# One room for all weight tiles, side work at fixed places, and unsplit last tiles in a two-layer trunk with experts

## The chip, the core and the metric

The kernel runs on one core of a Trainium2 chip. The metric is the device time of one execution in microseconds. A core has a matrix engine (TensorE, PE in the profile, with its weight loads as PEld), a vector engine (VectorE, DVE), a scalar engine (ScalarE, ACT), GpSimd (POOL) and SyncE (SP), which here only starts transfers. Each engine goes through its own list of instructions in order and waits for others by semaphores. Sixteen DMA engines carry the transfers.

## The reference

256 tokens of width 1024 go through two layers. Each has a mixer (four kinds of attention side by side, `w_in` and `w_out`) and a feed-forward part. In layer 0 that is dense, in layer 1 each token goes to 2 of 8 experts:

```
def swiglu(t, w_gate, w_up, w_down):
    return (jax.nn.silu(t @ w_gate) * (t @ w_up)) @ w_down

def moe_swiglu(h, router, w_gate, w_up, w_down):
    t = h.reshape(B * S, D)
    logits = (t @ router).astype(jnp.float32)
    top_val, top_idx = lax.top_k(logits, TOP_K)
    gates = jax.nn.softmax(top_val, axis=-1)
    combine = jnp.sum(jax.nn.one_hot(top_idx, N_EXPERTS) * gates[..., None], axis=1)
    out = jnp.zeros_like(t)
    for e in range(N_EXPERTS):
        out = out + combine[:, e:e + 1] * swiglu(t, w_gate[e], w_up[e], w_down[e])
```

Everything is float32; D = 1024, the hidden width F = 3584. A last RMSNorm follows. The experts' weights alone are 8 x 3 x 1024 x 3584 x 4 bytes, 352 MB of the 430 MB that the program reads.

## The kernel before

**Tiles and halves.** All large weights are a list of tiles, `units`, numbered in the order of use. The experts' part begins at tile 72. The hidden width of an expert is worked on in two halves of 1792, so there are 16 halves, i = 0 to 15. `expert_units` (L107) lists for each half eight gate tiles and eight up tiles (128 rows x 1792, 896 KB each) and then the seven down tiles (256 x 1024, 1 MB) of the half before. So half 0 is tiles 72 to 87, half 1 is 88 to 103, the down tiles of half 0 are 104 to 110, and so on; half 15's down tiles stand alone at the end and are cut finer (five whole ones and three pieces of 512 columns with 4, 2 and 2 row blocks).

**What is done to a tile.** A tile comes as float32 into a stage. For fp16 products it is split: ACT writes hi = fp16(512 w) (`high_part`, L169), DVE writes lo = fp16(512 w - hi) (`low_part`, L172). Tokens are split likewise, so each 128x128 block of weights takes three fp16 products with 96 token columns: hi with both parts of the tokens (L1157, L1158), lo with the first (L1161). In the down stage these are L1190 and L1192. The last gate tile and the last up tile of a half (`k == KD - 1`) are not split: TensorE multiplies them as float32 (L1151), which a record shows as two products for a block.

**Places.** Nine ring buffers (`stgp`, 8,320 bytes a partition) and four fixed places (e0, e2, e3, xn: buffers of earlier stages, 8,192 bytes) hold raw tiles, six hi and six lo buffers (`cvtp`) hold split ones. `load_next` (L156) starts one transfer on SP each time a raw place becomes free: after a tile's lo, or, for a tile that isn't split, after its products. A tile that leaves a fixed place hands it to the next tile in the list.

**What sets the order.** The schedule is manual: each engine's order is the order in which the code issues. `done` (L228) ends a tile's use and lets `go` split on until `ahead` tiles (six in the experts' part, `N_CVT`) are split past the one in use. The last nine tiles (`brisk`) are split in two pieces each.

**Around the tiles.** `gate_up` (L1164) does a half's gate and up tiles, then DVE and ACT finish the hidden values in three column spans: product (L1178), its fp16 part (L1179), the rest (L1180); this is "the three-part step". `down` (L1196) multiplies the half before. Other experts' side work is in a queue `side`: for the next expert, `slots` and five gathers of its tokens (copies at L1087); for the expert before, two transposes of its sum (`turn_back`, L1213 to L1216) and four additions into x (`scatter`, L1222 on TensorE, L1224 on DVE). One entry is taken after each up tile from the sixth on and after each down tile. `closing` (L1291) does the down tiles of half 15, the last transposes (tags e0, e1 : `yte`), additions and sums of squares. The final gain is loaded into a ring buffer after the last tile.

Of the kernel before, what the change touches and what calls it, by code (L numbers as in the profile page):

```python
# [20 lines left out]
P = 128  # L21
# [20 lines left out]
NB = FH // P  # L42

# [26 lines left out]
def hybrid_trunk_kernel(ctx: ExitStack, tc: tile.TileContext, a: dict, out: bass.AP, dbg=None):  # L70
# [4 lines left out]
    stgp = ctx.enter_context(tc.tile_pool(name="stgp", bufs=N_STG))  # L75
    cvtp = ctx.enter_context(tc.tile_pool(name="cvtp", bufs=N_CVT))
# [30 lines left out]
    def expert_units(sets, tail=False):  # L107
# [3 lines left out]
        for i in range(len(seq) + 1):  # L111
# [4 lines left out]
            if i > 0:  # L116
                (_, _, wd), h = seq[i - 1]
                ends = tail and i == len(seq)
                got += [(rows(wd, h * FH + r * P, 2, 0, D), 2, D, False) for r in range(0, NB - 4 if ends else NB, 2)]
                if ends:  # L120
                    r0 = h * FH + (NB - 4) * P
                    got += [(rows(wd, r0 + r * P, kt, c0, 512), kt, 512, False) for r, kt, c0 in ((0, 4, 0), (0, 2, 512), (2, 2, 512))]
        return got

    MLA_KT = (2, 2, 4)
    units = []
    for layer in range(DEPTH):
# [10 lines left out]
        if layer % 2 == 0:  # L138
            units += dense_units(a["dense_w_gate"][j], a["dense_w_up"][j], a["dense_w_down"][j])
        else:  # L140
            sets = [(a["moe_w_gate"][j, e], a["moe_w_up"][j, e], a["moe_w_down"][j, e]) for e in range(NE)]
            units += expert_units(sets, layer == DEPTH - 1)

    class Stream:


        def __init__(self, units, stage_tile, part_tiles, ahead):
            self.units, self.stage_tile, self.part_tiles = units, stage_tile, part_tiles
            self.loaded = self.split = self.low = self.used = 0
            self.stage, self.place, self.high, self.ready = {}, {}, {}, {}  # L150
# [3 lines left out]
            self.brisk = 0  # L154

        def load_next(self, place=None):  # L156
            u = self.loaded
            if u < len(self.units):
                src, kt, n, _ = self.units[u]
                stg = self.stage_tile(u, place)  # L160
                self.place[u] = place
                nc.sync.dma_start(stg[:, : kt * n].rearrange("p (k n) -> p k n", k=kt), src)
                self.stage[u] = stg
                self.loaded += 1
            elif place is None and self.last:
                self.last.pop()()
# [7 lines left out]
        def split_next(self):  # L174
# [7 lines left out]
            m = self.units[u][1] * self.units[u][2]  # L182
            self.high[u] = self.part_tiles[0](u)
            self.split += 1
            if u >= len(self.units) - self.brisk:
                self.low_until(u)
                lo = self.part_tiles[1](u)
# [8 lines left out]
        def top_up(self):  # L196

            if self.split < min(len(self.units), self.used + N_CVT) and not self.units[self.split][3]:
                u = self.split
                self.high[u] = self.part_tiles[0](u)  # L200
                self.high_part(u, slice(0, self.units[u][1] * self.units[u][2]))
                self.split += 1

        def low_until(self, end):
            while self.low < end:
                if self.units[self.low][3]:
                    self.ready[self.low] = (self.stage[self.low],)
                    self.low += 1
                    continue
                lo = self.part_tiles[1](self.low)  # L210
                self.low_part(self.low, lo, slice(0, self.units[self.low][1] * self.units[self.low][2]))
                self.low_done(lo)

        def low_done(self, lo):
            u = self.low
            _, kt, n, _ = self.units[u]
            self.stage.pop(u)
            self.ready[u] = tuple(z[:, : kt * n].rearrange("p (k n) -> p k n", k=kt) for z in (self.high.pop(u), lo))
            self.low += 1
            self.load_next(self.place.pop(u))  # L220

        def get(self, later=0):
            while self.split <= self.used + later:
                self.split_next()
# [3 lines left out]
        def done(self):  # L228
# [3 lines left out]
            if self.units[u][3]:  # L232
                self.stage.pop(u)
                self.load_next(self.place.pop(u))
# [6 lines left out]
        def go(self):  # L241
            while not self.held and self.split < min(len(self.units), self.used + self.ahead):
                self.split_next()
# [10 lines left out]
    parts = (  # L254
        lambda u: cvtp.tile([P, 2080], F16, tag="hi", name=f"hi{u}"),
        lambda u: cvtp.tile([P, 2080], F16, tag="lo", name=f"lo{u}"),
    )

    def stage_tile(u, place):
        if place:  # L260
            return (ext if place[0] == "e" else com).tile([P, 2048], F32, tag=place, name=f"stg{u}")
# [1141 lines left out]
```

## Time and profile before

| | |
|---|---|
| Time, median of 3 | 1368.21 us (1367.33 to 1368.56) |
| Profiled execution, its own time | 1368.37 us |
| Its span | 1366.6 us |
| PE, PEld busy | 1277.3 us (93%), 1134.5 us (83%) |
| DVE, ACT busy | 1079.5 us (79%), 898.2 us (66%) |
| POOL busy | 32.4 us (2%) |
| Read from memory | 430.41 MB, 316 GB/s over the span |

The span lies 1.77 us below the execution's own time. The busy shares are means over stages of different kinds: the first layer and the second layer's mixer up to about 500 us, the experts from there to 1347 us, and a short end of additions and the last norm. The experts' part is to be read by itself, in windows, and its two ends apart from its middle.

### The profile page before, as it was taken

Reading aid. Unit: us, or ns where it says so; the run is one execution under the profiler, and the core shown is the slowest. Engines: PE = TensorE matmul, PEld = TensorE weight load, DVE = VectorE, ACT = ScalarE, POOL = GpSimd, SP = SyncE. Lnnn points to the kernel's source line nnn. Section 1 sums busy time; section 2 is a strip of 40 time slices with the busy share of each in tenths; the row PEclk is TensorE's granted clock in tenths of the full one; section 3 lists DMA queues with packets and bytes.
Section 4 is the critical chain, followed back from the end, with each engine's and each line's share of the span. In section 5 each row is a group of like instructions: output and inputs, shape, how many; then the busy total and the mean of one; then the engine's idle time right before and its main releaser. Section 6 shows DMA issues by size and latency. Waiting matters only on the chain.

```text
span 1366.6 us, 43224 instructions
## 1 busy us (share of the span) xinstructions
PE 1277.3 (93%) x19680; PEld 1134.5 (83%) x19680; DVE 1079.5 (79%) x1032; ACT 898.2 (66%) x916; POOL 32.4 (2%) x51
## 2 busy tenths in 40 slices
PE   8999999999999998999999998998998998999885
PEld 5785877777587688999989988998998998999874
DVE  6655775666564587899998898898898998989976
ACT  6554654444544576788777678677777776877764
POOL 2300000000010010000000000000000000000000
PEclk9999999999999999999999999999999999999998
DMA  9953475646443459999999999999999999999991
GB/s 272 353 171 124 155 247 198 203 149 203 156 172 111 175 196 392 400 406 414 413 411 416 412 412 416 411 411 412 408 414 402 403 416 408 410 405 407 412 361 57
DMA packets 128799, 434.35 MB, mean 318 GB/s; under 512 B 11936, under 2 KB 59440, under 8 KB 128480
## 3 DMA queue, kind: packets, MB, share of 16 engines
q1 hardware_dynamic: 126640, 429.72, 81.4%
q8 instruction: 156, 2.56, 0.8%
q0 software_dynamic: 928, 1.78, 0.5%
q14 instruction: 35, 0.29, 0.1%
q10 hardware_dynamic: 1040, 0.00, 0.0%
HBM read 430.41 MB, written 1.06 MB: 316 GB/s over the span
## 4 chain that ended last, share of the span: by engine, by line
PE 23%; DMA 19%; DVE 11%; issue 5%; ACT 3%; SPq 0%; DVEq 0%; ACTq 0%
DMA stg<-in_moe_w_down_dram 13%; DVE lo L172 8%; PE my L1190 5%; DMA stg<-in_moe_w_up_dram 3%; DMA stg<-in_moe_w_gate_dram 3%; PE mu L1151 2%; PE my L1192 2%; PE mg L1161 2%; PE mg L1158 2%; PE mg L1157 2%; PE mg L1151 1%; ACT hi L169 1%; PE mu L1158 1%; PE mu L1157 1%; PE mu L1161 1%
## 5 line engine op out<-in xcount | busy, mean ns | idle before, releaser
L172 DVE SCALAR_TENSOR_TENSOR lo<-stg,hi 128x1792 f16<-128x1792 f32 (+3 forms) x418 | 849.4, 2078 | 44.0 <-ACT hi L169 43.8
L169 ACT ACTIVATE hi<-stg 128x1792 f16<-128x1792 f32 (+3 forms) x418 | 714.4, 1738 | 154.0 <-DMA stg<-in_moe_w_down_dram 56.7
L1158 PEld LDWEIGHTS <-hi 128*128 128x128 f16 x3136 | 271.8, 98 | 11.3 <-issue 11.1
L1157 PEld LDWEIGHTS <-hi 128*128 128x128 f16 x3136 | 272.7, 99 | 4.2 <-issue 4.0
L1192 PE MATMUL my<-rest,hi 128*128 128x96 f16 x1792 | 182.9, 208 | 0.9 <-issue 0.9
L1190 PE MATMUL my<-rest,hi 128*128 128x96 f16 x1792 | 183.0, 208 | 0.3 <-issue 0.3
L1190 PEld LDWEIGHTS <-hi 128*128 128x128 f16 x1792 | 157.6, 99 | 6.2 <-issue 3.3
L1192 PEld LDWEIGHTS <-hi 128*128 128x128 f16 x1792 | 157.2, 99 | 4.1 <-issue 1.0
L1157 PE MATMUL mg<-xgh,hi 128*128 128x96 f16 x1568 | 151.3, 208 | 8.0 <-DVE x L1224 6.0
L1158 PE MATMUL mg<-xgl,hi 128*128 128x96 f16 x1568 | 151.5, 208 | 5.4 <-issue 5.3
L1161 PEld LDWEIGHTS <-lo 128*128 128x128 f16 x3136 | 146.3, 98 | 5.2 <-issue 3.5
L1157 PE MATMUL mu<-xgh,hi 128*128 128x96 f16 x1568 | 147.1, 206 | 0.1
L1158 PE MATMUL mu<-xgl,hi 128*128 128x96 f16 x1568 | 147.1, 206 | 0.0
L1190 PE MATMUL my<-rest,lo 128*128 128x96 f16 x1792 | 115.4, 208 | 7.9 <-DVE lo L172 7.2
L1190 PEld LDWEIGHTS <-lo 128*128 128x128 f16 x1792 | 89.6, 99 | 9.6 <-DVE lo L172 8.6
L1161 PE MATMUL mg<-xgh,lo 128*128 128x96 f16 x1568 | 86.7, 207 | 2.9 <-issue 2.9
L1161 PE MATMUL mu<-xgh,lo 128*128 128x96 f16 x1568 | 85.2, 206 | 0.1
L459 PEld LDWEIGHTS <-hi 128*128 128x128 f16 x640 | 62.6, 98 | 9.9 <-issue 2.7
L460 PEld LDWEIGHTS <-hi 128*128 128x128 f16 x640 | 62.6, 98 | 7.2
L461 PEld LDWEIGHTS <-lo 128*128 128x128 f16 x640 | 62.6, 98 | 7.2
L1179 ACT CAST rest<-sg 128x480 f16<-128x480 f32 (+1 forms) x48 | 27.1, 566 | 60.4 <-DVE sg L1178 60.4
L1151 PE MATMUL mu<-xr,stg 128*128 128x96 f32 x448 | 64.4, 312 | 0.0
(355 smaller groups left out, 1868.2 us busy)
## 6 DMA issues: line engine op xcount, KB each, us to landing
stg<-in_moe_w_gate_dram SPq DMA_DIRECT2D x128, 896.0 KB, 17.9
stg<-in_moe_w_up_dram SPq DMA_DIRECT2D x128, 896.0 KB, 17.4
stg<-in_moe_w_down_dram SPq DMA_DIRECT2D x111, 1024.0 KB, 19.2
stg<-in_w_in_dram SPq DMA_DIRECT2D x14, 1024.0 KB, 7.0
stg<-in_dense_w_gate_dram SPq DMA_DIRECT2D x14, 1024.0 KB, 6.5
stg<-in_dense_w_up_dram SPq DMA_DIRECT2D x14, 1024.0 KB, 5.1
stg<-in_dense_w_down_dram SPq DMA_DIRECT2D x14, 1024.0 KB, 5.0
stg<-in_w_out_dram SPq DMA_DIRECT2D x8, 1024.0 KB, 9.0
```

Of the source, the lines that this page charges most:

```text
L169: se.activation(self.high[u][:, c], self.stage[u][:, c], AF.Copy, scale=SW)
L172: ve.scalar_tensor_tensor(lo[:, c], self.stage[u][:, c], SW, self.high[u][:, c], op0=OP.mult, op1=OP.subtract)
L459: te.matmul(ps, lh, rh, start=first, stop=False)
L460: te.matmul(ps, lh, rl, start=False, stop=False)
L461: te.matmul(ps, ll, rh, start=False, stop=last)
L1151: te.matmul(ps[b][:, c * C : (c + 1) * C], w[0][:, j * P : (j + 1) * P], xr, start=False, stop=ends and j + 1 == spans[b][1])
L1157: te.matmul(dst, L, xh[:, k, :], start=k == 0 and c == 0, stop=False)
L1158: te.matmul(dst, L, xl[:, k, :], start=False, stop=False)
L1161: te.matmul(ps[b][:, c * C : (c + 1) * C], lo[:, j * P : (j + 1) * P], xh[:, k, :], start=False, stop=ends and j + 1 == spans[b][1])
L1179: se.copy(hi[:, c], sg[:, c])
L1190: te.matmul(dst, W, L[0], start=first and part == 0 and d % 4 == 0, stop=ends and part == 1 and d % 4 == 3)
L1192: te.matmul(dst, W, L[1], start=False, stop=False)
```

## The change

**Places.** The ring and the hi and lo buffers are replaced by one tile `room` of the same bytes (N_STG x 8320 + N_CVT x 8320 = 124,800 a partition) and a list of free stretches, `Room`, kept while the program is written. `take` gives the first stretch that fits: a raw tile from the low end up to an edge, hi and lo as one pair (or two pieces) from the high end down to it. Before the experts' part each piece has the old size and the edge stands at 74,880 bytes; an expert's tile takes only its own bytes (7,168 for a gate or up tile, 8,192 for a down tile) and the edge is at 11 x 7,168 = 78,848. If no stretch fits, the load or the split waits for a later place in the order. The four fixed places stay.

**Splits ahead.** At half 3 (`i == 3`) `ahead` goes from six to three, and `lean` moves the edge to 124,800 - 4 x 8,192 = 92,032 bytes.

**Side work.** `slots` is done at the start of an even half; each other entry carries a number and is done after that tile (`beside`): gathers at 5, 7, 9, 11 and 13, where 5 and 7 are up tiles by `k` and 8 + n is the down tile n, both counted from 0, returns at 5, 6, 9, 10, 11, 12.

**The last half.** Half 15's down tiles are five whole ones, as before, and now five pieces of 512 columns (`ENDS`: 2, 2, 2, 1 and 1 row blocks). Two of the tiles (r = 2 and 6) and the pieces (0, 12), (512, 10), (512, 13) are left unsplit (`WHOLE`) and multiplied as float32 with `sg`, which ACT scales by 512 for that. The first transpose stands after the fourth of the five pieces, where it stood after the second of three.

```diff
@@ places
+ROOM = N_STG * 8320 + N_CVT * 8320
+EDGE = N_STG * 8320
+EDGE_X = 11 * FH * 4
+ENDS = ((0, 10, 2), (0, 12, 2), (512, 10, 2), (512, 12, 1), (512, 13, 1))
+WHOLE = (2, 6, (0, 12), (512, 10), (512, 13))
-    stgp = ctx.enter_context(tc.tile_pool(name="stgp", bufs=N_STG))
-    cvtp = ctx.enter_context(tc.tile_pool(name="cvtp", bufs=N_CVT))
+    room = cst.tile([P, ROOM // 4], F32, name="room")
+    class Room:
+        def __init__(self):
+            self.free = [(0, ROOM)]
+        def take(self, size, below, edge):
+            for a, b in self.free if below else self.free[::-1]:
+                lo, hi = (a, min(b, edge)) if below else (max(a, edge), b)
+                if hi - lo >= size:
+                    at = lo if below else hi - size
+                    self.free.remove((a, b))
+                    self.free += [z for z in ((a, at), (at + size, b)) if z[1] > z[0]]
+                    self.free.sort()
+                    return at, size
+            return None
@@ class Stream
+        def edge(self, u):
+            return ROOM - 4 * 8192 if self.lean else EDGE_X if u >= self.narrow else EDGE
         def load_next(self, place=None):
+            if place or self.stage_tile:
+                stg = (self.stage_tile or own_tile)(u, place)
+            else:
+                got = places.take(self.size(u) * 4 if u >= self.narrow else 8320, True, self.edge(u))
+                if got is None:
+                    return False
+        def part_tile(self, u, low):
+            size = self.size(u) * 2 if u >= self.narrow else 4160
+            if not low:
+                pair = places.take(2 * size, False, self.edge(u))
...
+        def stage_free(self, u):
+            self.stage.pop(u)
+            place = self.place.pop(u)
+            if place or self.stage_tile:
+                self.load_next(place)
+            else:
+                places.give(self.held_by[u].pop(0))
+            while self.stage_tile is None and self.load_next():
+                pass
@@ the halves
+        def beside(side, at):
+            while side and side[0][0] <= at:
+                side.popleft()[1]()
...
-                if k > 4 and side:
-                    side.popleft()()
+                beside(side, k)
...
+                if i == n_half - 1 and tag == "":
+                    se.activation(sg[:, c], sg[:, c], AF.Copy, scale=SW)
...
+                    if len(w) == 1:
+                        te.matmul(dst, W, sg[:, at_r], start=False, stop=ends and d % 4 == 3)
+                        continue
...
-                side.append(lambda e=e: slots(e + 1))
-                side.extend(gathers(e + 1))
+                slots(e + 1)
+                side.extend(zip((5, 7, 9, 11, 13), gathers(e + 1)))
             if i % 2 == 1 and e > 0:
-                side.extend(returns(e - 1))
+                side.extend(zip((5, 6, 9, 10, 11, 12), returns(e - 1)))
+            if i == 3:
+                stream[0].ahead = stream[0].most = 3
+                stream[0].lean = True
```

On DVE, where half 15's up tiles end, expert 6's transposed sum (`back`, `yt60` and `yt61`), the splits of down tiles of half 14 (429 to 431), the first addition (`st6_00`) and the three-part step (`mu15`, `sg`, `rest1`) stand like this before:

```order
L1216 TENSOR_TENSOR back_4985<-yt60_22431,back_4985 96x512
L172 SCALAR_TENSOR_TENSOR lo429_22482<-stg429_21883,hi429_22425 128x2048
L1216 TENSOR_TENSOR back_4985<-yt61_22486,back_4985 96x512
L172 SCALAR_TENSOR_TENSOR lo430_22509<-stg430_21975,hi430_22480 128x2048
L1224 SCALAR_TENSOR_TENSOR x_80<-st6_00_22511,share_4967,x_80 128x512
L1178 SCALAR_TENSOR_TENSOR sg_4986<-mu15_0_22146,sg_4986 128x480
L1180 TENSOR_TENSOR rest1_4984<-sg_4986,rest_4983 128x480
```

And now, with the tiles' places all called `room`:

```order
L1307 TENSOR_TENSOR back_4744<-yt60_21288,back_4744 96x512
L252 SCALAR_TENSOR_TENSOR room_58<-room_58 128x2048
L1307 TENSOR_TENSOR back_4744<-yt61_21340,back_4744 96x512
L252 SCALAR_TENSOR_TENSOR room_58<-room_58 128x2048
L1264 SCALAR_TENSOR_TENSOR sg_4745<-mu15_0_21011,sg_4745 128x480
L1266 TENSOR_TENSOR rest1_4743<-sg_4745,rest_4742 128x480
```

The addition has left its place ahead of the three-part step. On TensorE at the same place, from the last products of the up tile 425 (L1151, L1233 in the new code), the rows before are:

```order
L1151 MATMUL mu15_2_22148<-xr7_19044,stg425_21676 128x96 x4
L1222 LDWEIGHTS peT6_17045
L1222 MATMUL st6_00_22511<-back_4985,peT6_17045 128x512
L1222 LDWEIGHTS peT6_17045
L1222 MATMUL st6_00_22511<-back_4985,peT6_17045 128x512
L1190 LDWEIGHTS hi426_22285
L1190 MATMUL my14_0_22524<-rest_4983,hi426_22285 128x96
```

And now:

```order
L1233 MATMUL mu15_0_21011<-xr7_17464,room_58 128x96 x5
L1233 MATMUL mu15_1_21012<-xr7_17464,room_58 128x96 x5
L1233 MATMUL mu15_2_21013<-xr7_17464,room_58 128x96 x4
L1281 LDWEIGHTS room_58
L1281 MATMUL my14_0_21375<-rest_4742,room_58 128x96
```

TensorE goes from the up tile straight into the first down tile (`my14`); the addition's products stand after the second. On DVE at the end of the program, the splits of the last tiles (434 to 440) up to the last transposes (`yte`) are before:

```order
L1224 SCALAR_TENSOR_TENSOR x_80<-st6_11_22698,share_4967,x_80 128x512
L172 SCALAR_TENSOR_TENSOR lo435_22751<-stg435_22141,hi435_22750 128x1024 x2
L172 SCALAR_TENSOR_TENSOR lo436_22805<-stg436_22195,hi436_22804 128x1024 x2
L172 SCALAR_TENSOR_TENSOR lo437_22859<-stg437_22241,hi437_22858 128x1024 x2
L172 SCALAR_TENSOR_TENSOR lo438_22913<-stg438_22333,hi438_22912 128x1024 x2
L172 SCALAR_TENSOR_TENSOR lo439_22969<-stg439_22381,hi439_22968 128x512 x2
L172 SCALAR_TENSOR_TENSOR lo440_23023<-stg440_22429,hi440_23022 128x512 x2
L1216 TENSOR_TENSOR back_4985<-yte0_23246,back_4985 96x512
```

And now:

```order
L1315 SCALAR_TENSOR_TENSOR x_75<-st6_11_21639,share_4726,x_75 128x512
L252 SCALAR_TENSOR_TENSOR room_58<-stg433_21058,room_58 128x2048
L252 SCALAR_TENSOR_TENSOR room_58<-stg435_21149,room_58 128x1024 x2
L252 SCALAR_TENSOR_TENSOR room_58<-room_58 128x1024 x2
L252 SCALAR_TENSOR_TENSOR room_58<-room_58 128x512 x2
L252 SCALAR_TENSOR_TENSOR room_58<-room_58 128x256 x2
L1307 TENSOR_TENSOR back_4744<-yte0_21988,back_4744 96x512
```

Of the last tiles' splits five rows are left after the addition, the first of them in one piece.

## Rows read from the trace of the kernel before

**Rows 1.** The page's slices: the span in 40 parts, DMA share and rate

```profile
DMA  9953475646443459999999999999999999999991
GB/s 272 353 171 124 155 247 198 203 149 203 156 172 111 175 196 392 400 406 414 413 411 416 412 412 416 411 411 412 408 414 402 403 416 408 410 405 407 412 361 57
```

**Rows 2.** Windows: stretch, length, busy PE, PEld, DVE, ACT, POOL, PE's clock, DMA share, GB/s

```profile
541.00:557.00 16.00, 16.00 (x330) 16.00 (x328) 12.40 (x8) 13.51 (x10) 0.00 (x0) 0.99 0.95 345
645.00:1285.00 640.00, 593.45 (x12031) 580.74 (x12028) 581.71 (x379) 481.97 (x365) 0.00 (x0) 0.97 1.02 411
1308.00:1314.00 6.00, 0.90 (x5) 0.27 (x4) 5.05 (x4) 5.00 (x4) 0.00 (x0) 0.90 1.01 408
1314.00:1319.00 5.00, 5.00 (x52) 4.17 (x52) 5.00 (x4) 3.58 (x3) 0.00 (x0) 0.50 1.01 388
1322.00:1338.00 16.00, 16.00 (x373) 15.76 (x371) 14.79 (x15) 14.80 (x17) 0.00 (x0) 1.00 0.68 247
1338.00:1347.00 9.00, 8.72 (x187) 8.11 (x185) 9.00 (x11) 3.43 (x6) 0.00 (x0) 1.00 0.01 2
```

**Rows 3.** Waits of SP's queue, 645 to 1285 us: total us, count, longest

```profile
SPq L162 <- DVE lo L172: 154.2, 110, 5.0
SPq L162 <- DMA stg<-in_moe_w_gate_dram: 129.3, 84, 1.9
```

**Rows 4.** Timeline of SP: start, length, loads of half 0's down tiles

```profile
527.23 0.97 SPq L162 DMA_DIRECT2D stg<-in_moe_w_down_dram  x2
...
537.36 0.37 SPq L162 DMA_DIRECT2D stg<-in_moe_w_down_dram  x1
...
545.04 0.37 SPq L162 DMA_DIRECT2D stg<-in_moe_w_down_dram  x1
```

**Rows 5.** Timeline of DVE between half 0 and half 1: start, length, operation

```profile
525.18 2.02 DVE L172 SCALAR_TENSOR_TENSOR lo<-stg,hi 128x1792 f16<-128x1792 f32 x1
527.11 0.65 DVE L1178 SCALAR_TENSOR_TENSOR sg<-mu,sg 128x480 f32<-128x480 f32 x1
...
534.35 1.01 DVE L1087 CAST xgl<-gx 128x384 f16<-128x384 f32 x2
535.28 2.02 DVE L172 SCALAR_TENSOR_TENSOR lo<-stg,hi 128x1792 f16<-128x1792 f32 x1
...
542.99 5.90 DVE L172 SCALAR_TENSOR_TENSOR lo<-stg,hi 128x1792 f16<-128x1792 f32 x3 [1.34 <-ACT hi L169]
```

**Rows 6.** Timeline of DVE in the tail, rows of like splits merged (x3, x12)

```profile
1319.45 0.64 DVE L1178 SCALAR_TENSOR_TENSOR sg<-mu,sg 128x480 f32<-128x480 f32 x1
...
1324.81 4.55 DVE L172 SCALAR_TENSOR_TENSOR lo<-stg,hi 128x2048 f16<-128x2048 f32 x3
...
1329.95 2.35 DVE L172 SCALAR_TENSOR_TENSOR lo<-stg,hi 128x1024 f16<-128x1024 f32 x2
...
1335.81 11.57 DVE L172 SCALAR_TENSOR_TENSOR lo<-stg,hi 128x1024 f16<-128x1024 f32 x12
```

**Rows 7.** The chain that ended last: start, length, engine, tile and line

```profile
1128.34 3.17 PE mg L1151 x28
...
1327.11 0.38 PE my L1190 x9
...
1346.90 0.46 PE yte L1213 x4
```

**Rows 8.** Timeline of ACT: the hi of the tail's first tile, with its wait

```profile
1303.17 1.91 ACT L169 ACTIVATE hi<-stg 128x2048 f16<-128x2048 f32 x1 [3.32 <-DMA stg<-in_moe_w_down_dram]
```

**Rows 9.** DVE by form, 647.7 to 1288.4 us: busy, mean ns, idle before, releaser

```profile
L172 DVE SCALAR_TENSOR_TENSOR lo<-stg,hi 128x2048 f16<-128x2048 f32 x84 | 191.8, 2287 | 22.2 <-ACT hi L169 22.0
L1224 DVE SCALAR_TENSOR_TENSOR x<-st,share,x 128x512 f32<-128x512 f32 x24 | 17.9, 744 | 0.0
L1180 DVE TENSOR_TENSOR rest<-sg,rest 128x480 f16<-128x480 f32 x24 | 15.8, 659 | 23.8 <-ACT rest L1179 23.8
L1216 DVE TENSOR_TENSOR back<-yt,back 96x512 f16<-96x512 f32 x12 | 8.2, 683 | 3.7 <-ACT back L1215 3.7
```

More of the change, by code (lines that the diff above doesn't have):

```diff
@@ new lines, in part_tile @@
+        def part_tile(self, u, low):
+            size = self.size(u) * 2 if u >= self.narrow else 4160
+            if not low:
+                pair = places.take(2 * size, False, self.edge(u))
+                both = [(pair[0], size), (pair[0] + size, size)] if pair else [places.take(size, False, self.edge(u)) for _ in range(2)]
+                if not all(both):
+                    for got in filter(None, both):
+                        places.give(got)
+                    return None
+                self.held_by.setdefault(u, []).extend(both)
+            return at(self.held_by[u][low - 2], F16)
@@ L199, in top_up @@
                 u = self.split
-                self.high[u] = self.part_tiles[0](u)
-                self.high_part(u, slice(0, self.units[u][1] * self.units[u][2]))
-                self.split += 1
+                hi = self.part_tile(u, 0)
+                if hi is not None:
+                    self.high[u] = hi
+                    self.high_part(u, slice(0, self.size(u)))
+                    self.split += 1
         def low_until(self, end):
@@ L232, in done @@
             if self.units[u][3]:
-                self.stage.pop(u)
-                self.load_next(self.place.pop(u))
+                self.stage_free(u)
+            else:
+                for got in self.held_by.pop(u):
+                    places.give(got)
             if self.later:
@@ L1203, in down @@
                 unit_done()
[L1204 to L1205 removed]
+                beside(side, KD + r // 2)
         def finish(acc, n):
@@ L1233, in final_gain @@
         def final_gain():
-            fin["g"] = stgp.tile([P, 2080], F32, tag="stg", name="final_gain")[:, :D]
-            nc.sync.dma_start(fin["g"], spread(a["final_norm"], D))
+            got = places.take(D * 4, True, EDGE_X)
+            if got:
+                fin["g"] = at(got, F32)
+                nc.sync.dma_start(fin["g"], spread(a["final_norm"], D))
+            return got
         stream[0].last.append(final_gain)
@@ L1337, in moe @@
             else:
-                while side:
-                    side.popleft()()
+                beside(side, 99)
             assert not side
```

119 lines of the change are left out of this document (69 added, 50 removed).

## The prediction

> **What bounds the kernel now.** I read the slices of the page first, then the stage of the experts alone, then its two ends. The slices [rows 1] show three kinds of time: up to slice 15 the DMA engines are half idle, from there to slice 38 they are full at some 400 to 416 GB/s, and the last slice has almost none. So the stage of the experts is a stream of weights, and only three things can shorten it: more tiles loaded before the stream starts, holes closed in it, or a shorter tail behind it.
>
> The stretches [rows 2] say that of the stream's middle nothing can be had. From 645 to 1285 us the DMA share is 1.02 at 411 GB/s, while PE is busy for 593 and DVE for 582 of 640 us. The queue's own waits there [rows 3] are long, but a good part of them is for DMAs, that is for the oldest of eight loads in flight: the loads stand in line, not the line waiting for loads. At 411 GB/s a gate or up tile (896 KB) takes 2.23 us and a down tile (1 MB) 2.55 us; a half of an expert, 16 and 7 of them, takes 53.5 us. DVE does 582/12 = 48.5 us of work in each of the twelve halves there: full, but not the bound.
>
> There is one hole. From 541 to 557 us the rate falls to 345 GB/s [rows 2]. The rows around it say why. Half 0 has no down tiles behind its up tiles, so DVE goes from its last split (525.18) straight into the three-part step that finishes the hidden values (527.11) and the shares, then copies the next expert's tokens (534.35), and only then splits again (535.28) [rows 5]. Each split frees a place for a load; the loads of the first down tiles go out at 527.23 (two), 537.36 and 545.04 [rows 4], the last only when the three splits from 542.99 have begun to end.
>
> The tail is DVE's. From 1322 to 1338 us the rate falls to 247 GB/s as the last loads run out, from 1338 to 1347 us nothing lands and DVE is busy for 9.00 of 9.00 us [rows 2]. It splits the last tiles until 1347.4 [rows 6], and TensorE's transpose of the finished sum starts at 1346.90 [rows 7], 19.7 us before the end.
>
> **More places.** Gate and up tiles now take 7,168 bytes a partition and not 8,320, and the part of the room below the edge holds eleven of them, not nine. By the code's own arithmetic the last tile loaded ahead of the pause before 497 us is two further on, so at the restart two tiles of 2.23 us have landed already: a gain of 4.5 us, if the stream never has to wait for places afterwards. I followed the places through the first halves. The third of the seven down tiles of half 0 goes out after the split that ends about 527, the fourth after that of 535.28, the fifth, in the room as in the ring, only when the first up tile of half 1 has been split: its 8,192 bytes fit none of the holes that gate tiles leave, and it takes one of the four fixed places. That split is one of the three from 542.99, and its load went out at 545.04 [rows 4]. The stream, two tiles ahead, runs through the third and fourth by about 542 and then has nothing in flight until 545. The lead is spent there: the fifth lands as before, the sixth and seventh some 0.3 us later, since they go out together, after one more split than before. From then on both kernels stream at the same rate. So I book +0.3 us for the room, with bounds of -4.5 us (lead kept) or -6.5 us (the hole also closed, 16 us at 345 instead of 411 GB/s, 2.6 us, less what instructions' own loads take of it) and +1 us. I take the upper end since the gap in DVE's rows ahead of 535.28 is the three-part step and the copies, and both stay. Only slots moves out of this piece, two operations of 0.2 us.
>
> **Side work at fixed places.** The step that puts an expert's result back waits for DVE behind splits that wait for loads; TensorE then stands, as from 1308 to 1314 us, where it is busy for 0.90 of 6 us, and is granted half its clock until 1319 (0.50) [rows 2]. Its moves take such stands away, once in a half, some 5 us each. In the stream that is worth nothing: TensorE is busy 593 of 640 us and the loads are the bound. In the tail it is worth nothing either, since DVE ends last there. Nothing, then, from -1 to +1 us.
>
> **Three tiles ahead.** From half 3 on a tile's first half (hi) is written when TensorE has finished the tile three before, not six, and the raw places grow by the difference. The stream needs no more raw places; the question is whether DVE still keeps up. Its spare time per half is 53.5 - 48.5 = 5.0 us, of which the three-part step takes 2 in waits for ACT (23.8 us in twelve halves before its largest operation alone) [rows 9]. The closer coupling costs DVE a wait behind each unsplit tile (ACT has to wait 3.2 us for TensorE, DVE has two splits of 2.0 us to fill them, then a hi of 1.7 us to wait for): below 1 us, twice a half. 48.5 + 2.6 + 1.8 = 52.9 us, under 53.5 by a hair. I book nothing, with +6 us (half a microsecond in each of 13 halves) as the bound above.
>
> **Unsplit last tiles.** Of the last half's seven down tiles 3.25 are no longer split. DVE is spared 3.25 x 2.3 = 7.5 us (the two halves of one tile take 2.35 us at 1329.95) [rows 6]. TensorE pays: a block of 128x128 weights takes three fp16 products of 42 ns (nine in 0.38 us) [rows 7], 0.127 us, but as fp32 a pair of products, 28 for 14 blocks in 3.17 us [rows 7], 0.226 us. 52 blocks more at 0.099 us are 5.1 us. TensorE's slack to DVE in the tail is smaller: from the first tile's split (1332.3) it had 32 products of that tile, 1.36 us, four tiles of 2.04 us and 1.5 tiles more, 12.6 us in all, where the transpose came after 14.6 us. So 2 us are hidden and about 3 us are not.
>
> The same from the front. The first tile of the tail is ready for DVE at 1305.1 (its hi starts at 1303.17) [rows 8]. Up to the last half's first down tile DVE has eight splits of 2.2 us (the three rows' worth of 4.55 us at 1324.81 are one whole tile and two halves, 2.35), two copies (0.68), four additions (0.74), and the three-part step, 5.4 us from 1319.45 to 1324.81 [rows 6, 9]: 17.6 + 1.3 + 2.9 + 5.4 = 27.2 us, 1332.3, as now. The step comes three splits earlier, which changes the order and not the sum. From there TensorE has 1.36 us, then unsplit 3.62, split 2.04, unsplit 3.62, split 2.04, 1.02, unsplit 1.81 and 1.81, split 0.51: 17.8 us, and the transpose stands at 1350.1 instead of 1346.9. That is +3.2 us. Bounds: +0.8, if DVE loses its 2.4 us of waits before 1332, and +4.5, if TensorE, which now stands near 1314 to 1319 for the third tile's split, runs at half its clock behind it.
>
> The rows price an fp32 block at 0.226 us [rows 7]. The Trainium skill would price it otherwise: "FP8 and Floating Point Precision", TensorE Precision Notes, gives a true fp32 product four passes through the array; by that page a block of 96 columns would be an estimated 4 x 40 = 160 ns, and the tail's 3.2 us would shrink to about half a microsecond. The trace of before disagrees with it, by 0.226 us.
>
> **The sum.** 0.3 for the room, 0 for side work and for three ahead, 3.2 for the tail: 1366.6 + 3.5 = 1370.1 us of span. The profiled execution took 1368.37 us, 1.77 us over its span and 0.16 us over the median of 1368.21. So 1370.1 + 1.77 - 0.16 = 1371.7 us.
>
> **The rivals.** First, the lead of two tiles is kept, because the splits of half 1 come earlier than I think or the fifth load finds a place. Then the stream ends 4.5 to 6.5 us earlier, and with the tail's +0.8 to +3.2 the time is 1362.5 to 1367, most likely 1365. For it speaks that the hole is only some 3 us long, against it that DVE's order up to 535.28 is unchanged. Second, DVE becomes the bound from half 3 on, where a wait of more than 0.6 us a half is added to my 52.9: 3 to 7 us on top of the forecast, 1375 to 1379 us. For it speaks how little spare there is, against it that two raw places more absorb a late stretch. Third, the unsplit tiles cost less in the tail than the pairs of the up stage: if a block of 96 columns took four passes of 42 ns [rows 7], 0.17 us, TensorE would need from 1332.3 on 1.36, 2.72, 2.04, 2.72, 2.04, 1.02, 1.36, 1.36 and 0.51, 15.1 us, the transpose would stand at 1347.4, 0.5 us later than now, and the time would be 1369.0 us. Against it speak the 113 ns for each of the 28 products of the same kind [rows 7]. This is also what the four passes of the Trainium skill would give.
>
> **How the numbers follow.** The bound for a difference that can be told is 0.2%, 2.7 us. Forecast 0.43, its own range 1369 to 1374; of it 0.31 slower by more than that, 0.12 within. Lead kept 0.28: 0.22 faster, 0.06 within. DVE the bound 0.17, slower. Cheap unsplit tiles 0.12: 0.09 within, 0.03 faster, since a part of the lead may come to it. Faster 0.25, same 0.27, slower 0.48. Cases of both signs hold much of this, so the range goes from 1363 to 1378: about 0.1 of the first rival lies below it, and 0.08 of the second and worse above.
>
> **What would show it.** In the profile of the changed kernel: the rate between 541 and 557 us again below 400 GB/s, with the fifth load of a down tile at 545 (right) or none below 400 (wrong: the lead is kept). From 645 to 1285 us a rate of 410 GB/s or more (right), or DVE busy all the time with the rate below 408 (three ahead is too few). No stand of TensorE before the addition of the other expert's result, and one before the third down tile's split instead. In the tail, DVE done 8 us or more before the transpose and TensorE's fp32 pairs back to back at 0.226 us. My forecast is wrong if the transpose starts before 1347 us.

## The result and the profile after

The changed kernel takes 1380.75 us (median of five, 1377.35 to 1384.54), the kernel before 1368.21 beside it: a ratio of 1.0091, 95% interval 1.0079 to 1.0103. It is slower, as forecast, but by 12.5 us where 3.5 were forecast, and above the range. Its profiled execution took 1381.08 us, with a span of 1379.2.

The page's row of rates by slice (GB/s) and the same stretches as in [rows 2], with one more behind them (1347 to 1360 us) and the columns given there:

```profile
GB/s 271 370 147 123 154 244 198 200 159 203 175 138 161 188 217 328 398 408 415 417 411 415 414 398 416 412 397 416 412 413 415 409 401 414 411 402 413 412 271 33
541.00:557.00 16.00, 16.00 (x333) 16.00 (x331) 13.31 (x7) 12.94 (x11) 0.00 (x0) 1.00 0.65 224
645.00:1285.00 640.00, 588.16 (x11827) 573.58 (x11825) 575.20 (x376) 478.80 (x361) 0.00 (x0) 0.97 1.02 410
1308.00:1314.00 6.00, 5.97 (x135) 5.85 (x132) 4.39 (x4) 4.13 (x4) 0.00 (x0) 1.00 1.02 406
1314.00:1319.00 5.00, 5.00 (x72) 5.00 (x69) 4.70 (x4) 4.19 (x3) 0.00 (x0) 1.00 1.03 408
1322.00:1338.00 16.00, 11.74 (x186) 10.33 (x183) 14.55 (x12) 11.71 (x10) 0.00 (x0) 0.79 0.74 281
1338.00:1347.00 9.00, 9.00 (x164) 9.00 (x161) 8.08 (x7) 4.36 (x5) 0.00 (x0) 1.00 0.03 8
1347.00:1360.00 13.00, 13.00 (x198) 13.00 (x194) 2.05 (x4) 3.65 (x6) 0.00 (x0) 1.00 0.01 1
```

The stream is as long as it was. Its restart is the first load that SP has sent out after the pause: at 497.3 us before, at 498.9 after (over all runs this point lies between 496 and 500.5, whatever the kernel). Counted from there, the last load lands 839.1 us later before and 839.2 after. From 645 to 1285 us the rate is 410 GB/s against 411. All that is lost, but for the later restart, comes after the last landing: the transpose of the last sum (from its weight load on) stood 10.3 us behind it, now 21.4.

The chain that ended last, from 1317.74 us on (start, length, what), and ACT's timeline at the first down tile of half 14 show two pieces of this:

```profile
1317.74 2.28 DVE room L252
...
1325.33 2.30 DVE room L252
1327.67 0.90 PE my L1281 x9
...
1343.19 3.61 PE my L1279 x32
...
1348.84 3.61 PE my L1279 x32
...
1355.51 3.61 PE my L1279 x32
...
1359.64 0.46 PE yte L1304 x4
```

```profile
1311.54 1.91 ACT L249 ACTIVATE room<-room 128x2048 f16<-128x2048 f32 x1 [1.70 <-PE mu L1240]
```

Before, this tile's hi started as it landed, at 1303.2, and ACT had waited for it [rows 8]. Now it landed at 1303.6 and its hi starts at 1311.54, after a wait for TensorE: the computing runs 8 us behind the stream when the stream ends. The second piece is in the three float32 stretches (L1279), 3.61 us for 16 blocks each.

How far the computing is behind can be read from the trace for each tile: the start of its hi less its landing. Here this is called the backlog. For the first gate tile of four halves and for the first down tile of half 14 (a tile at the head of the tail), in us:

| | half 4 | half 7 | half 10 | half 13 | last down | time |
|---|---|---|---|---|---|---|
| before | 7.2 | 4.7 | 5.5 | 5.3 | 0.1 | 1368.2 |
| after | 13.7 | 14.1 | 15.7 | 13.6 | 8.0 | 1380.8 |

At half 3 both have 11 us, left over from the start. Before, about half of this melts in two halves, and at the first down tile of half 14 nothing is left; after, it stays to the end. A half of computing (hi to hi, mean from half 4 to 13) takes 54.2 us after, and a half of the stream (landing to landing) 54.2 too: the backlog has no difference to melt by. What a half of computing takes when it does catch up, the experiments show: 53.1 to 53.4 us with three tiles ahead.

### The profile page after: what moved, and what is told of

Same layout as the page of the kernel before. It is cut to its first block, busy times and chain, and to the rows that moved or that the text cites. A ratio compares the mean times of both kernels' runs of the same rounds, so it can differ in the third digit from the quotient of the medians.

```text
span 1379.2 us, 43089 instructions
## 1 busy us (share of the span) xinstructions
PE 1285.5 (93%) x19628; PEld 1141.1 (83%) x19628; DVE 1073.6 (78%) x1024; ACT 894.0 (65%) x911; POOL 32.4 (2%) x51
## 4 chain that ended last, share of the span: by engine, by line
PE 36%; DMA 9%; DVE 9%; ACT 3%; issue 2%; DVEq 0%; ACTq 0%; SPq 0%
PE my L1281 7%; DVE room L252 6%; PE mg L1243 4%; DMA room<-in_moe_w_gate_dram 4%; PE mg L1239 4%; PE mg L1240 4%; PE mg L1233 3%; PE mu L1239 3%; PE mu L1240 3%; PE my L1283 3%; PE mu L1243 3%; DMA room<-in_moe_w_up_dram 2%; DMA stg<-in_moe_w_down_dram 2%; ACT room L249 2%; DMA stg<-in_moe_w_gate_dram 1%
## 5 line engine op out<-in xcount | busy, mean ns | idle before, releaser
L252 DVE SCALAR_TENSOR_TENSOR room<-room 128x1792 f16<-128x1792 f32 (+4 forms) x312 | 645.4, 2097 | 90.6 <-ACT room L249 88.7
L249 ACT ACTIVATE room<-room 128x1792 f16<-128x1792 f32 (+4 forms) x312 | 542.8, 1758 | 248.3 <-issue 62.5
L1281 PE MATMUL my<-rest,room 128*128 128x96 f16 x3480 | 252.6, 213 | 50.4 <-DVE room L252 50.2
L1281 PEld LDWEIGHTS <-room 128*128 128x128 f16 x3480 | 241.4, 102 | 57.3 <-DVE room L252 52.5
L1240 PEld LDWEIGHTS <-room 128*128 128x128 f16 x3136 | 271.1, 98 | 11.7 <-issue 11.5
L1239 PEld LDWEIGHTS <-room 128*128 128x128 f16 x3136 | 271.9, 98 | 2.7 <-issue 2.6
L252 DVE SCALAR_TENSOR_TENSOR room<-stg,room 128x1792 f16<-128x1792 f32 (+2 forms) x98 | 203.7, 2095 | 9.1 <-ACT room L249 8.6
L249 ACT ACTIVATE room<-stg 128x1792 f16<-128x1792 f32 (+2 forms) x98 | 170.6, 1756 | 35.4 <-PE mg L1240 9.5
L1283 PE MATMUL my<-rest,room 128*128 128x96 f16 x1740 | 185.4, 212 | 0.0
L1283 PEld LDWEIGHTS <-room 128*128 128x128 f16 x1740 | 159.4, 102 | 4.2 <-issue 1.5
L1239 PE MATMUL mg<-xgh,room 128*128 128x96 f16 x1568 | 150.1, 207 | 10.4 <-DVE xgl L1169 6.3
L1240 PE MATMUL mg<-xgl,room 128*128 128x96 f16 x1568 | 150.3, 207 | 2.2 <-issue 2.0
L1243 PEld LDWEIGHTS <-room 128*128 128x128 f16 x3136 | 146.0, 98 | 5.9 <-DVE room L252 1.6
L1239 PE MATMUL mu<-xgh,room 128*128 128x96 f16 x1568 | 147.1, 206 | 0.4 <-issue 0.4
L1240 PE MATMUL mu<-xgl,room 128*128 128x96 f16 x1568 | 147.1, 206 | 0.0
L1243 PE MATMUL mg<-xgh,room 128*128 128x96 f16 x1568 | 86.6, 207 | 1.4 <-DVE room L252 1.0
L1243 PE MATMUL mu<-xgh,room 128*128 128x96 f16 x1568 | 85.1, 206 | 0.0
L541 PEld LDWEIGHTS <-room 128*128 128x128 f16 x640 | 62.8, 98 | 9.9 <-issue 2.7
L542 PEld LDWEIGHTS <-room 128*128 128x128 f16 x640 | 62.8, 98 | 7.4
L543 PEld LDWEIGHTS <-room 128*128 128x128 f16 x640 | 62.8, 98 | 7.4
```

The costliest lines, as they stand in the source:

```text
L249: se.activation(self.high[u][:, c], self.stage[u][:, c], AF.Copy, scale=SW)
L252: ve.scalar_tensor_tensor(lo[:, c], self.stage[u][:, c], SW, self.high[u][:, c], op0=OP.mult, op1=OP.subtract)
L541: te.matmul(ps, lh, rh, start=first, stop=False)
L542: te.matmul(ps, lh, rl, start=False, stop=False)
L543: te.matmul(ps, ll, rh, start=False, stop=last)
L1239: te.matmul(dst, L, xh[:, k, :], start=k == 0 and c == 0, stop=False)
```

## The experiments

All times are medians; ratios are to the kernel before, run beside each.

**Which part costs it.** Four variants of the changed kernel: six tiles ahead to the end; the side work one entry after each tile, as before; all last tiles split; and the first and the third together.

```diff
-            if i == 3:
-                stream[0].ahead = stream[0].most = 3
-                stream[0].lean = True
```


> The changed kernel without the step at half 3: six tiles ahead and the old edge to the end. Theory A (the closer coupling keeps the backlog between landing and split that the start leaves, and the tail pays it): the backlog melts by about half 5, the first down tile of half 14 is split within 1 us of its landing and not 8 us behind it, and the time falls by those 8 us to 1371 to 1374. Theory B (the fixed places of the side work make TensorE stand) and theory C (the unsplit last tiles cost all of it): no change, 1379 to 1382.


1374.3 us, 1.0046 (1.0030 to 1.0063), just above theory A's range: 6.4 us come from the step at half 3, where 8 were expected. The backlog is 7.1, 2.6, 4.4, 3.5 and 0.1 in the table's columns. ACT's row at the first down tile has it waiting for the load again:

```profile
1301.65 1.91 ACT L249 ACTIVATE room<-room 128x2048 f16<-128x2048 f32 x1 [2.27 <-DMA room<-in_moe_w_down_dram]
```


```diff
-                beside(side, k)
+                if k > 4 and side:
+                    side.popleft()[1]()
```


> The changed kernel with the side work taken one entry after each tile from the sixth up tile on, as before. Theory A: the stand of TensorE behind the three-part step stays at some 3.5 us a half, and the time at 1379 to 1383. Theory B: TensorE's waits for DVE in the down stage go from 46 us to under 15 and the time falls to 1371 to 1374. Theory C: no change.


(The same after down tiles, and `slots` back in the queue.) 1379.8 us, 1.0087 (1.0070 to 1.0104). Theory B falls: TensorE's waits for DVE in the down stage are 43.9 us from 645 to 1285, where the changed kernel has 46.0.

```diff
-WHOLE = (2, 6, (0, 12), (512, 10), (512, 13))
+WHOLE = ()
```


> The changed kernel with every tile of the last half split. DVE then has about 14.8 us of splits after the first down tile of the last half (1341.5 in the profile of the changed kernel), so it ends near 1356 and the transpose stands near 1357.5 instead of 1359.6. Theory A: 1377 to 1380, about 2 us gained, since behind a late DVE the unsplit tiles cost less than in my forecast. Theory C (unsplit tiles are the loss): 1368 to 1370.


1377.7 us, 1.0066 (1.0049 to 1.0083): 3.1 us less than the changed kernel, in theory A's range.

> Both: six tiles ahead to the end and all tiles of the last half split; room and side work as in the changed kernel. Theory A with my term of 3.2 us for the tail: the time before plus the 1.4 us by which the stream ends later, 1368.5 to 1370.5. If room or side work lost time by themselves it would stay above 1372.


1369.7 us, 1.0013 (1.0003 to 1.0023): 4.6 us less than with six ahead alone. The step at half 3 and the unsplit tiles together are 11.0 of the 12.5 us; what is left of the change (room, side work) costs 1 to 2 us here.

**Three ahead.** Then the step at half 3 by itself, in the ring; taken back at half 12; with four instead of three; and without the move of the edge.

```diff
 # kernel before
+            if i == 3:
+                stream[0].ahead = stream[0].most = 3
```


> The kernel before with nothing but three tiles ahead from half 3 on: its ring, its side work, its tail with all tiles split. Theory A (three ahead stops the backlog from melting, whatever the places are): TensorE stands for DVE about 3.5 us once in a half, the first down tile of half 14 is split 6 to 10 us behind its landing, and the time is 1375 to 1379. If three ahead needs the new room or the new side order to do harm: 1367 to 1371.


1366.9 us, 0.9990 (0.9980 to 0.9999). A miss: theory A in this form falls. In the ring three ahead does no harm; the backlog is 11.7, 7.2, 3.4, 2.6, 0.1, and a half of computing takes 53.3 us, 1 us less than the stream's. ACT's waits for hi, 645 to 1285 us (total, times, longest), are for loads, while TensorE waits for DVE in the down stage:

```profile
ACT hi L169 <- DMA stg<-in_moe_w_up_dram: 21.4, 23, 2.8
ACT hi L169 <- DMA stg<-in_moe_w_down_dram: 18.8, 14, 3.7
```

```profile
PE my L1190 <- DVE lo L172: 41.3, 27, 5.6
```

The kernel before has 6.9 us of these waits. So three ahead does cost TensorE a stand of some 3 us a half, in the ring as in the room (46.0 us in the changed kernel), but the ring's halves stay short enough to catch up.


```diff
+            if i == 12:
+                stream[0].ahead = stream[0].most = N_CVT
+                stream[0].lean = False
```


> The changed kernel, with six tiles ahead and the old edge again from half 12 on. Theory A: the nine halves with three ahead cost nothing by themselves, since the stream runs on; the backlog of 14 us melts at some 4.5 us a half in the last four, and the time is that of six ahead throughout, 1373 to 1376. Theory D (three ahead slows every half a little): nine of twelve parts of the 6.4 us stay, 1378 to 1380.


1374.5 us, 1.0043 (1.0030 to 1.0056). The backlog, 11.7 us at half 12, is 0.1 at the last down tile. The slow halves cost nothing until the stream ends; theory D falls.

```diff
-                stream[0].ahead = stream[0].most = 3
-                stream[0].lean = True
+                stream[0].ahead = stream[0].most = 4
```


> The changed kernel with four tiles ahead from half 3 on and the old edge. Theory A: the stand behind the three-part step shrinks by one tile of 2.04 us, so a half takes some 52.3 us of computing against 54.2 of the stream, the backlog melts by half 10 and the time is 1373 to 1376, as with six. If every tile less ahead cost alike, two of the three steps from six to three would stay: 1378 to 1379.


1372.7 us, 1.0029 (1.0018 to 1.0041), just below theory A's range; the backlog is down to 1.8 us at half 7.

```diff
-                stream[0].lean = True
```


> The changed kernel with three tiles ahead from half 3 on, but the edge left at 78,848 bytes, so some 11 expert tiles below it and not 12.8. Theory A: the number ahead does the harm and not the added raw places; the stream is full either way, 1379 to 1382. If the deeper line of raw tiles were the cause (more tiles landed and waiting at the end): 1375 to 1378, since 1.4 tiles less can wait.


1380.2 us, 1.0079 (1.0063 to 1.0096). The edge doesn't matter.

**Ring or side work.** Since three ahead costs 6 us in the changed kernel and nothing in the ring, the ring got the new side work, and the room the old.

> The kernel before with two parts of the change, three tiles ahead from half 3 on and the fixed places of the side work; ring and split tail as before. Theory E (with three ahead a half's computing takes 53.3 us with the old places and 54.2 with the new ones, against 54.3 of the stream, so the backlog melts with the old and stays with the new): the backlog in front of the down tiles stays at 8 to 12 us to the end, the time is 1374 to 1379. Theory F (the room, not the places of the side work, makes the difference to three ahead alone): 1366 to 1369, with the backlog gone by half 11.


1367.9 us, 0.9991 (0.9981 to 1.0000), backlog 10.6, 7.0, 3.3, 1.6, 0.1. Theory E falls: the places of the side work are harmless with three ahead too.

> The changed kernel with the side work as before and all last tiles split: so room and three ahead alone, where the ring with three ahead took 1366.9. Theory E: 0.7 us a half melt, but the backlog at half 4 is 6 us larger than in the ring, so some 5 us of it are left: 1371 to 1374. Theory F: 1374 to 1378. If the room is neutral: 1367 to 1369.


1376.9 us, 1.0057 (1.0039 to 1.0074), backlog 18.3, 16.0, 15.9, 15.3 and 10.2. It is the room. A half of computing takes 53.8 us with this order of the side work, so some of the backlog melts, but it starts higher and the tail still pays 10 us.

**What of the room.** From half 3 on `take` lays a pair into the highest free stretch. Following the list of free stretches through the code (the numbers of pairs come from there and not from a trace), about 90 of 100 pairs then come to lie on bytes of the tile three before, the last to be left; and since pairs of up tiles are 7,168 bytes and those of down tiles 8,192, they shift against each other, so that in about a third the new hi lies on an old lo. TensorE reads lo last, by the order of its products. ACT's waits in the changed kernel, 645 to 1285 us (total, times, longest), and TensorE's longest:

```profile
ACT room L249 <- PE mg L1240: 30.7, 22, 5.7
ACT room L249 <- PE mu L1240: 25.4, 23, 1.7
ACT room L249 <- PE my L1283: 22.9, 43, 1.1
ACT room L249 <- PE my L1281: 19.8, 12, 2.0
ACT room L249 <- PE mu L1243: 8.2, 12, 1.2
...
ACT room L249 <- PE mg L1243: 2.4, 6, 0.5
```

```profile
PE my L1281 <- DVE room L252: 46.0, 13, 4.2
```

These are 109 us of ACT's waits for TensorE, at 118 of some 250 tiles. Four runs take this apart: pairs in turn over five places of 8,192 bytes; the ring with three of its six buffers; pairs in turn over three places; and the highest free stretch with all pairs of 8,192 bytes, so that hi lies on hi.

```diff
...
+                if self.lean:
+                    pair = places.take_at(ROOM - (self.turn % 5 + 1) * 8192, 2 * size)
+                    self.turn += 1
...
```


> The changed kernel with three tiles ahead and the edge at 78,848, as in the run that took 1380.2, and one thing more: from half 3 on a pair of hi and lo goes in turn to one of five places of 8,192 bytes above the edge, and not into the highest free stretch, which is the one that the tile three before has just left. Theory G (the highest free stretch makes six pairs into three, so that hi of a tile waits until TensorE has finished the tile three before): ACT's waits for TensorE go from 100 us to under 20, the backlog melts and is gone at the last down tiles, the time is that of six ahead with the unsplit tail, 1371 to 1375. If three ahead in the order of the program is the cause by itself: 1379 to 1382.


1372.6 us, 1.0030 (1.0020 to 1.0041), 7.6 us less than with the same edge and the highest stretch; backlog 9.1, 5.2, 1.4, 1.0, 0.1. ACT now waits mostly for loads again (L263 is its line here):

```profile
ACT room L263 <- DMA stg<-in_moe_w_down_dram: 11.9, 7, 3.0
ACT room L263 <- DMA stg<-in_moe_w_up_dram: 10.9, 9, 2.7
...
ACT room L263 <- PE my L1297: 7.3, 13, 0.8
```

```diff
 # kernel before, three ahead from half 3, pools of three
+        side = "" if few.get("on") or few[what] % 6 < 3 else "2"
+        return cvtp.tile([P, 2080], F16, tag=what + side, name=f"{what}{u}")
...
```


> The kernel before with three tiles ahead from half 3 on, and from there on only three of its six hi and lo buffers in use; ring, side work and tail as before. With all six in use it took 1366.9. Theory G: ACT waits for TensorE some 8 us a half, the backlog of 12 us in front of half 4 stays, the time is 1374 to 1379. If the room does it in another way: 1366 to 1368.


1367.4 us, 0.9993 (0.9984 to 1.0003). A miss for theory G: three pairs alone do no harm, though ACT waits for TensorE there too (54 us, the largest row below). The backlog melts more slowly (14.7, 8.6, 5.9, 3.4, 0.1), but in time.

```profile
ACT hi L169 <- PE my L1196: 38.9, 52, 1.9
```

```diff
...
+                    pair = places.take_at(ROOM - (self.turn % 3 + 1) * 8192, 2 * size)
...
```


> As the run with pairs in turn, but over three places and not five. By the list of places 71 of 100 tiles after half 3 then get the bytes of the tile three before, as in the ring with three buffers, the others, next to unsplit tiles, those of the tile four before, and hi always lies on an earlier hi. Theory G (three pairs are too few): 1378 to 1381. Theory H (hi on the lo of the tile three before, which TensorE reads last, or the loss of the slack at unsplit tiles): 1372 to 1376, with the backlog melting at about 1 us a half as in the ring with three.


1371.8 us, 1.0024 (1.0014 to 1.0034), backlog 12.8, 7.1, 5.7, 2.2, 0.1. So it is not the number of pairs. That hi always lies on an earlier hi, as the expectation says, is not quite so: where down tiles follow up tiles, a hi of 4,096 bytes reaches past an older one of 3,584 onto its lo. These are a few tiles a half, and ACT's waits for lo products stay at some 3 us.

```diff
...
+            size = 4096 if self.lean else self.size(u) * 2 if u >= self.narrow else 4160
```


> The highest free stretch is taken as in the changed kernel, with three ahead and the edge at 78,848 (that run took 1380.2), but every pair after half 3 takes 8,192 bytes, whatever the tile, so that hi never lies on an earlier lo (in the changed kernel it does for 32 of 100 tiles). 85 of 100 tiles still get the bytes of the tile three before. If hi on lo is the harm: 1372 to 1376. If it is the choice of the highest free stretch, which leaves the slack at unsplit tiles unused: 1378 to 1381.


1373.1 us, 1.0026 (1.0015 to 1.0038), against 1380.2 with pairs by size; backlog 14.2, 9.0, 9.5, 4.1, 0.1. ACT's waits, 645 to 1285 us:

```profile
ACT room L249 <- PE my L1283: 38.1, 54, 2.1
ACT room L249 <- PE mg L1240: 30.4, 22, 4.0
ACT room L249 <- PE mu L1240: 12.1, 21, 1.1
```

The last products that read a hi are L1240 and L1283, the last that read a lo L1243 and L1281. The waits for lo products (30.4 us above) are gone, those for hi products stay, 81 us against 79. A half of computing falls from 54.2 to 53.2 us. So what costs the time is that pairs of two sizes shift against each other in the highest free stretch; the choice of that stretch and the small number of pairs leave enough to melt the backlog. That it costs by hi landing on lo is what the waits say; equal pairs also keep a pair from covering two older ones, which by the list happens to nearly the same pairs, and no run separates the two.

> The same with pairs in turn, and all tiles of the last half split: the changed kernel without its two losses. Theory G and the tail's 4 us by the unsplit tiles: 1366.5 to 1370.


1367.5 us, 0.9991 (0.9982 to 1.0001): the changed kernel without its two losses can't be told from the kernel before.

**Two more.** Three ahead only for the last halves, and the high edge with three ahead where places are short:

```diff
 # kernel before
+            if i == 14:
+                stream[0].ahead = stream[0].most = 3
```


> The kernel before with three tiles ahead only from half 14 on. The profile of three ahead from half 3 on has its last transpose 8.3 us behind the last landing, against 10.3 before. If that is the closer coupling in the tail: 1365.5 to 1367.5. If it was the stream's luck in that run: 1368 to 1369.5.


1366.6 us, 0.9990 (0.9980 to 1.0000). The transpose stands 8.5 us behind the last landing (10.3 before; 8.3 with three ahead from half 3): with three ahead the three-part step comes some 10 us earlier on DVE, at 1309.34 against 1319.45 [rows 6]. It is the likeliest reason of a gain that the times hardly show.

```diff
-        stream[0].ahead = stream[0].most = N_CVT
+        stream[0].ahead = stream[0].most = 3
+        stream[0].lean = True
...
             if i == 3:
-                stream[0].ahead = stream[0].most = 3
-                stream[0].lean = True
+                stream[0].ahead = stream[0].most = N_CVT
+                stream[0].lean = False
```


> The changed kernel turned round: three ahead and the high edge in halves 0 to 2, where raw places are short, six ahead and the old edge from half 3 on, all last tiles split. If the hole at 541 to 557 us is one of places that down tiles do not fit, one or two loads go out some 4 us earlier there, the last load lands 2 to 4 us earlier and the time is 1366 to 1368. If the hole is the pause in DVE's splits, three ahead moves nothing: 1369 to 1371, as with six ahead and the split tail (1369.7).


1376.1 us, 1.0054 (1.0034 to 1.0074): worse than either. The hole is shallower, 337 GB/s from 541 to 557 us where the changed kernel has 224, but half 2 of computing takes 52.1 us and not 48.2, at a time when loads wait for places that computing frees; the last load lands 844.5 us after the restart and not 839.2. At the start three ahead with the high edge costs stream, behind half 3 it costs backlog.

## Why the prediction was wrong, step by step

**The stream and the lead: right.** SP's timeline has the four loads into fixed places in one row. The last of them, the fifth down tile, which no hole of the room fits, is out at 530.32 + 16.42 = 546.7, 47.8 us after the restart (545.4 and 48.1 before [rows 4]), and the next two follow after one more split:

```profile
530.32 16.42 SPq L220 DMA_DIRECT2D stg<-in_moe_w_down_dram  x4
551.73 0.88 SPq L220 DMA_DIRECT2D room<-in_moe_w_down_dram  x2
```

The two tiles of lead are spent in the hole, as booked, and it is deeper for them (224 GB/s where it was 345). Booked +0.3, measured +0.1. That these are so near is in part luck: counted from the restart, the seventh down tile lands 1.2 us later than before and not 0.3, and the stream makes this up afterwards, by some 0.1 us a half, for a reason that stays open. The first rival did not come.

**Side work: right.** TensorE's stand at 1308 to 1314 is gone (5.97 us busy and not 0.90). As the prediction said, one before a down tile's split has come in its place, behind the three-part step: of the 16 us from 1322 TensorE is idle for 4.3, until DVE's split of 1325.33 lets it go on at 1327.67. It is worth nothing: in the ring with three ahead the kernel takes 1367.9 us with the new places and 1366.9 with the old.

**Three tiles ahead: the step that failed.** I wrote 48.5 + 2.6 + 1.8 = 52.9 us of DVE in a half, "under 53.5 by a hair", and booked nothing. Three things were wrong. The half of computing was too short, because waits were counted behind unsplit tiles only: with three ahead TensorE waits some 3.5 us for DVE once in a half, behind the three-part step (46.0 in 13), and in the room ACT waits for TensorE at nearly every second tile, 109 us in 640. A half took 54.2. The first of these waits is in the ring too (41.3), where a half took 53.3; the step to 54.2 goes with the pairs of two sizes in the highest free stretch, which the prediction didn't ask about. The half of the stream was too short as well: by landings it is 54.2 to 54.4 us and not 53.5, before as after. And I asked only whether the stream would be slowed. It wasn't; the second rival's price, 3 to 7 us of stream, did not come. What I left out is that the computing starts half 3 with 11 us of backlog and needs the difference between its half and the stream's to work it off. With 53.3 us a half (ring, three ahead) twelve halves are enough, with 54.2 they are not, and the tail pays 8 us. In the median that is 6.4 us with the unsplit tiles and 8.0 with all tiles split (1377.7 less 1369.7).

**Unsplit tiles: the price right, the size too small.** A block took 0.226 us as booked (3.61 us for 16), and the third rival, four passes of 42 ns, fell. The Trainium skill ("FP8 and Floating Point Precision", TensorE Precision Notes) gives four passes for true float32, by which the prediction estimated 0.16 us a block; the trace disagrees here too, by the 0.226 us. The term was 3.2 us; measured 4.6 with six ahead, 5.1 with pairs in turn (1372.6 less 1367.5), 3.1 in the changed kernel. My sum of 17.8 us ran from the split of the last half's first down tile and took TensorE to be waiting there. With six ahead its windows show it otherwise:

```profile
1320.00:1325.00 5.00, 1.01 (x16) 1.01 (x17) 4.21 (x5) 4.24 (x5) 0.00 (x0) 0.93 0.95 331
1325.00:1330.00 5.00, 4.38 (x47) 3.69 (x46) 5.00 (x4) 4.58 (x4) 0.00 (x0) 0.50 0.93 340
1330.00:1336.00 6.00, 6.00 (x125) 6.00 (x123) 6.00 (x7) 3.56 (x6) 0.00 (x0) 0.91 0.47 181
```

It stands 4 us for the split behind the three-part step, is granted half its clock until 1331, and reaches the first float32 product at 1335.55. DVE ends the split in question at 1331.5 in this run, so my sum would have had it at 1331.5 + 1.36 = 1332.9. That is the bound of +4.5 which I had named and not taken.

**The sum.** Of the profiled execution, 0.1 us is the stream's and 11.1 us are those by which the transpose is further from the last landing: 7.9 for the backlog (8.0 less 0.1), if all of it is paid, and 3.2 that are left for the rest of the tail. That these 3.2 are the number I had booked is chance, as the runs above show. Another 1.6 us of this execution are its later restart. The two losses don't add up: each taken out by itself gives back 6.4 and 3.1 us of the median, each put in by itself costs 8.0 and 4.6, and both together cost 11.0. The likely reason is that unsplit tiles spare a late DVE work; no run tests this by itself.

## What to carry to other kernels

Where one resource bounds a long stage, don't ask only whether a change slows that resource: ask how much backlog the stage starts with, and whether each round still works some of it off before the tail has to pay. When buffers come from a free list that is searched from one end and not from a ring, the last one left is often the first one taken, and pieces of different sizes come to lie on others' later halves; equal pieces or taking places in turn cost nothing here and gave 7 us back. A saving on one engine in the tail is to be priced from where the other engine really stands, with its clock after a wait.

## What the runs showed of the hardware

In all runs but one the stream's pace didn't depend on what SP waited for: a half took 54.1 to 54.4 us (landings, half 4 to 13), whether SP waited for loads [rows 3] or for places (366.7 us for DVE from 645 to 1285 us in the changed kernel). The exception is the run with three ahead at the start, where halves 3 and 4 of the stream took 56.5 us at 391 and 398 GB/s, and SP waited for hardly anything but DVE. TensorE was granted half its clock after its long stands in the tail: 0.50 from 1314 to 1319 us before, after the stretch with 0.90 us busy of 6 [rows 2], and 0.50 from 1325 to 1330 with six ahead, after a stand of 4 us. Else nothing unexpected.
